# A hybrid decoder layer on eight cores: retention chunks of 128, sums of squares moved off TensorE, four single PSUM side banks

## The chip, the cores and the metric

One Trainium2 chip, eight cores in two dies of four. Each core computes one of eight sequences; nothing is exchanged. The time is that of the slowest core, in device microseconds. All runs named here gave correct results.

The program runs in two states. In a **fast** run the cores have a mean granted TensorE clock that is mostly near 0.993 of full speed. In a **slow** run one die or both are granted less, down to 0.81, and the time is up to 19% longer. The verdict (faster, same, slower) uses fast runs alone. I also use the dies that were left alone: a die whose four cores all show a clock above 0.988 is called **undisturbed**, and its value is the span of its slowest core. Spans are some 2 us under the time.

## The reference, cut to what matters

```python
h = rmsnorm(x);  q_a,k_a,v_a,q_r,k_r,v_r,g_r,z_a,z_r = split(h @ w_in)      # 1024 -> 9472
A = sliding_window_attention(q_a, k_a, v_a)      # window 128, blocks of 128, a sink per head
R = silu(g_r) * rms_group_norm(retention(q_r, k_r, v_r))   # 4 heads, 256 x 512 state, decay gamma
x = x + (sigmoid(z_a) * (A @ w_ba) + sigmoid(z_r) * (R @ w_br)) @ w_out
x = x + (silu(g @ w_gate) * (g @ w_up)) @ w_down,   g = rmsnorm(x)          # FFN of 2816
```

Sequence length 8192, 16 tiles of 512 tokens per core. Retention is computed chunk by chunk with a running state, so the chunk length is the kernel's choice.

## The kernel before

The program lists its operations once, tile by tile: phase A (projections), side (attention and retention), phase F (the FFN of the tile before), phase G (gates, branches, output). A small list scheduler in the kernel file then orders each engine's stream, so side matmuls are fitted between the dense ones of A and F. Dense matmuls use four PSUM banks, side matmuls the other four, here as two double ones. Cut to the parts that the change touches:

```python
PP = Pool("PP", [pp[:, i, :] for i in range(2)])            # two side buffers of 1024 columns

def norm_fm(src, Rsrc, dst, Rdst, gain):                    # RMS norm, features on partitions
    pb = Buf(PP)
    for j in range(4):
        sq = Buf(T16);  act(sq.ap, src[:, 2*j:2*j+2, :], AF.Square, 1024)
        # two matmuls by a matrix of ones: 8 of 512 columns per norm
        S.op("pe", [mm(pb.ap[:, 0:512], ones, sq.ap[:, i*512:(i+1)*512], ...) for i in range(2)])
    ...
def ret_out(t, cc, h, inn):                                 # chunk cc of 256 tokens, head h
    for d in range(4):
        mm(oo(0, 256), vr[c0], inn[:, 0:256])               # inner part, first 128 keys
        mm(oo(128, 256), vr[c1], inn[:, 256:384])           # inner part, second 128 keys
        for dt in range(2): mm(oo(0, 256), Db[h, dt, d], qrT[:, 2*h+dt, 256 tokens])   # state part
    act(sq.ap, po.ap, AF.Square, 1024)
def ret_norm(t, cc, h, po, sq):                             # epsilon and four squares by ones
    fns = [mm(pb.ap[:, 0:256], ones, epsr[:, h, :])] + [mm(pb.ap[:, 0:256], ones, sq[d]) for d in range(4)]
def side(t):
    for (c, eg), (cc, h) in zip([(c, eg) for c in range(4) for eg in range(2)],
                                [(cc, h) for cc in range(2) for h in range(4)]):
        inn = ret_inner(t, cc, h);  km = ret_ktm(t, cc, h)
        pP, pC = attn_scores(t, c, eg);  attn_pv(t, c, eg, pP, pC)   # four pairs of half-array matmuls
        po, sq = ret_out(t, cc, h, inn);  ret_norm(t, cc, h, po, sq);  ret_upd(t, cc, h, km)
```

Weights come from HBM as float32. In the first pass GpSimd issues loads that cast to bf16 into a ring of seven units; each unit is then written back to a bf16 scratch, from which later passes load.

## Time and profile before

| | value |
|---|---|
| the three runs | 5723.11, 5725.18 and 6009.57 us |
| median of the three | 5725.18 us |
| profiled run | 5725.64 us, all clocks 0.991 to 0.994 |
| middle tile | 344.9 us on an undisturbed core, TensorE busy throughout |
| first output tile leaves | 623 to 646 us |

### The profile page before, as it was taken

Reading aid. Unit: us, or ns where it says so; the run is one execution under the profiler, and the core shown is the slowest. Engines: PE = TensorE matmul, PEld = TensorE weight load, DVE = VectorE, ACT = ScalarE, POOL = GpSimd, SP = SyncE. Lnnn points to the kernel's source line nnn. Section 1 sums busy time; section 2 is a strip of 40 time slices with the busy share of each in tenths; the row PEclk is TensorE's granted clock in tenths of the full one; section 3 lists DMA queues with packets and bytes.
Section 4 is the critical chain, followed back from the end, with each engine's and each line's share of the span. In section 5 each row is a group of like instructions: output and inputs, shape, how many; then the busy total and the mean of one; then the engine's idle time right before and its main releaser. Section 6 shows DMA issues by size and latency. Waiting matters only on the chain.

```text
span 5724.1 us, 68116 instructions; the slowest of 8 cores (5698.5 to 5724.1 us)
## 1 busy us (share of the span) xinstructions
PE 5524.7 (97%) x27957; PEld 2606.3 (46%) x28508; DVE 2451.2 (43%) x3550; ACT 2976.4 (52%) x4524; POOL 517.1 (9%) x461
## 2 busy tenths in 40 slices
PE   5788899999999999999999999999999999999999
PEld 2334344444444444444444444444444444444444
DVE  2425344353443535435353443535435344443533
ACT  2636345564454645545565454645546555455643
POOL 2021010100101001020010101001020010101000
PEclk9899999999999999999999999999999999999999
DMA  8676844435354354544535454353544535454353
GB/s 188 145 200 154 223 137 156 156 118 188 129 173 149 120 184 129 173 141 146 165 119 184 133 168 148 121 184 129 173 144 133 173 125 178 138 158 152 113 181 129
DMA packets 241080, 881.13 MB, mean 154 GB/s; under 512 B 26881, under 2 KB 26881, under 8 KB 240641
## 3 DMA queue, kind: packets, MB, share of 16 engines
q1 hardware_dynamic: 228386, 831.65, 44.6%
q0 software_dynamic: 12384, 45.09, 5.1%
q8 instruction: 225, 3.69, 0.3%
q14 instruction: 85, 0.70, 0.0%
HBM read 843.08 MB, written 78.64 MB: 161 GB/s over the span
## 4 chain that ended last, share of the span: by engine, by line
PE 91%; DMA 5%; ACT 2%; DVE 1%; issue 1%; POOL 0%; SPq 0%; POOLq 0%
PE pd L513 79%; PE pp L513 12%; DMA ring<-wpk 2%; ACT s L491 1%; DMA xs<-xT 1%; DMA ring<-wscr 1%; DMA wscr<-ring 1%; PE pp L745 0%; DMA retT<-cb 0%; ACT d L491 0%; DVE d L499 0%; DVE h L502 0%; DVE retT L499 0%; DVE Wst L502 0%; DVE qaT L499 0%
## 5 line engine op out<-in xcount | busy, mean ns | idle before, releaser
L513 PE MATMUL pd<-h,ring 128*128 128x512 bf16 x12589 | 2959.7, 380 | 46.8 <-issue 10.5
L513 PEld LDWEIGHTS pd<-h,ring 128*128 128x128 bf16 x12928 | 1233.6, 98 | 1514.1 <-issue 106.0
L491 ACT ACTIVATE d<-pd 128x512 f32<-128x512 f32 x864 | 509.5, 590 | 1348.0 <-PE pd L513 1344.6
L499 DVE TENSOR_TENSOR d<-pd,d 128x512 f32<-128x512 f32 x736 | 508.4, 691 | 1374.3 <-ACT d L491 793.5
L491 ACT ACTIVATE d<-d,cst_sb 128x512 f32<-128x512 f32 x864 | 623.1, 721 | 25.6
L513 PE MATMUL pd<-actb,ring 128*128 128x512 bf16 x2765 | 613.2, 380 | 13.4 <-DMA ring<-wpk 10.7
L491 ACT ACTIVATE d<-d 128x512 f32<-128x512 f32 x864 | 542.1, 627 | 22.1
L513 PE MATMUL pd<-ring,h 128*128 128x512 bf16 (+1 forms) x2506 | 500.7, 350 | 17.4 <-DMA ring<-wpk 14.5
L513 PE MATMUL pd<-retT,ring 128*128 128x512 bf16 x2015 | 461.6, 379 | 9.1 <-DMA ring<-wpk 7.3
L491 ACT ACTIVATE s<-pp 128x1024 bf16<-128x1024 f32 (+2 forms) x512 | 382.6, 755 | 163.3 <-PE pp L513 159.9
L499 POOL TENSOR_TENSOR qrT<-actb,d 128x512 bf16<-128x512 f32 x112 | 141.6, 1264 | 3579.8 <-DVE d L499 3579.7
L491 ACT ACTIVATE xs<-pd,cst_sb 128x512 bf16<-128x512 f32 x256 | 175.8, 687 | 497.6 <-PE pd L513 497.1
L513 PEld LDWEIGHTS pd<-actb,ring 128*128 128x128 bf16 x2816 | 275.2, 98 | 346.6 <-DMA ring<-wpk 15.5
L499 DVE TENSOR_TENSOR x<-pd,x 128x512 f32<-128x512 f32 x256 | 177.0, 691 | 585.5 <-PE pd L513 583.6
L499 DVE TENSOR_TENSOR actb<-pd,d 128x512 bf16<-128x512 f32 (+1 forms) x480 | 331.3, 690 | 179.0 <-PE pd L513 106.7
L513 PE MATMUL pp<-s,cb_sb 128*128 128x256 bf16 (+2 forms) x1423 | 309.1, 345 | 54.3 <-ACT mprev L491 34.5
L513 PEld LDWEIGHTS pd<-ring,h 128*128 128x128 bf16 x2560 | 233.6, 99 | 266.3 <-DMA ring<-wpk 16.9
L499 DVE TENSOR_TENSOR d<-pd,actb 128x512 f32<-128x512 f32 x512 | 329.0, 685 | 19.5 <-PE pd L513 8.5
L502 DVE SCALAR_TENSOR_TENSOR qaT<-pd,cst_sb,s 128x512 bf16<-128x512 f32 x128 | 95.5, 746 | 540.1 <-ACT s L491 540.1
L513 PEld LDWEIGHTS pd<-retT,ring 128*128 128x128 bf16 x2048 | 199.8, 98 | 250.5 <-DMA ring<-wpk 10.2
L491 ACT ACTIVATE s<-pp,cst_sb 128x512 f32<-128x512 f32 (+1 forms) x302 | 257.9, 855 | 62.2 <-PE pp L513 61.9
L499 POOL TENSOR_TENSOR krT<-d 128x512 bf16<-128x512 f32 x128 | 160.0, 1272 | 1084.0 <-DVE d L499 1084.0
(54 smaller groups left out, 3901.1 us busy)
## 6 DMA issues: line engine op xcount, KB each, us to landing
ring<-wscr SPq DMA_DIRECT2D x1290, 512.0 KB, 3.6
ring<-wpk POOLq DMA_DIRECT2D x86, 512.0 KB, 14.6
wscr<-ring SPq DMA_DIRECT2D x86, 512.0 KB, 12.3
xs<-xT SPq DMA_DIRECT2D x64, 512.0 KB, 5.7
x<-xT SPq DMA_DIRECT2D x64, 512.0 KB, 5.2
out<-x SPq DMA_DIRECT2D x64, 512.0 KB, 4.1
actb<-cs SPq DMA_DIRECT2D x16, 512.0 KB, 6.1
retT<-cb SPq DMA_DIRECT2D x1, 1024.0 KB, 26.5
```

What stands on the lines that cost most here:

```text
L491: return e.activation(out(), in_(), func, scale=scale, **kw)
L499: return S.op(eng, lambda e: e.tensor_tensor(out(), a(), b(), op), dur, reads, writes, cls=cls)
L502: return S.op("dve", lambda e: e.scalar_tensor_tensor(out(), a(), sc, b(), op0, op1), 0.067 + n / 960.0, reads, writes, cls=cls)
L513: return lambda e: e.matmul(out(), w(), r(), start=st, stop=sp)
```

## The change

The intent is to take array columns off TensorE, which is full, and give the small sums to engines that have room: retention chunks of 128 instead of 256, sums of squares added on GpSimd before one matmul by ones, softmax denominators from one VectorE sum. Four single side banks replace two double ones. The side jobs go by head pair. Half of the FFN weight units skip the write-back in the first pass and are cast again in the second. Since GpSimd now computes in several steps, two lines of the scheduler also make it wait, by semaphore, before it overwrites data of its own earlier instructions; they are not shown. The core of the diff, cut:

```diff
-        PP = Pool("PP", [pp[:, i, :] for i in range(2)])
+        PP = Pool("PP", [pp[:, i, :] for i in range(4)])          # pp is now [128, 4, 512]
 # RMS norms: after the first tiles, GpSimd adds the eight squares, one matmul by ones
+                lo, hi = sq.ap[:, 0:512], sq.ap[:, 512:1024]
+                acc = actb[:, 10, :];  tt("pool", acc, lo, hi, ALU.add, 512, ...)   # ... six more adds
+                        S.op("pe", mm(b.ap, ones, ss.ap[:, 0:512], True, True), ...)
+            norm_fm(xs, ..., g1, t <= 2)                            # True: the old way, on TensorE
+            norm_fm(x2, ..., g2, t == ntiles - 1 or t == 0)
 # softmax denominators
+            if t <= 1: return pP, pC, None
+            tt("dve", pS.ap, pP.ap, pC.ap, ALU.add, 1024, ...)      # then one pair by ones instead of two
 # retention: chunks of 128 tokens, two heads per job
-                fns.append(mm(oo(128, 256), vr[:, c1, ...], inn.ap[:, 256:384], ...))
-                        fns.append(mm(oo(0, 256), Db[...], qrT[:, 2 * h + dt, cc * 256:(cc + 1) * 256], ...))
+                        fns.append(mm(oo, Db[...], qrT[:, 2 * h + dt, c * 128:(c + 1) * 128], ...))
 # retention norm
+            if t <= 1: return po, sq
+            tt("pool", qf.ap, sq.ap[:, 0:256], sq.ap[:, 256:512], ALU.add, 256, [sq], [qf])
+            tt("pool", qf.ap[:, 0:128], qf.ap[:, 0:128], qf.ap[:, 128:256], ALU.add, 128, ...)
+            tt("pool", sb_.ap, qf.ap[:, 0:128], epsf[:, h, :], ALU.add, 128, ...)
-            fns = [ones x epsr] + [ones x sq[d] for d in range(4)]  # 5 matmuls of 256 columns
+                fns = [mm(pb.ap[:, 0:128], ones, sb_.ap, True, True)]
 # order of the side jobs
-            for (c, eg), (cc, h) in zip(jobs_a, jobs_r):
+            for eg in range(2):                                     # head pair 0,1 or 2,3
+                for c in range(4):
 # FFN weights: odd units are cast again in the second pass and written back only there
-        WF = Stream(NU_A)
+        WF = Stream(NU_A, True)
+                    late = self.half and u % 2 == 1
+                    if self.npass == 0 or (late and self.npass == 1):  # cast load
+                        if self.npass == (1 if late else 0):           # write back
```

## The prediction

> **What bounds the kernel now.** I read the page first: busy shares, then the waits of TensorE by stretch, then the timeline inside one stretch, then the groups by shape for what the side engines would pay.
>
> The page's first part, and two stretches of about one 512-token tile each in the middle, with the stretch views of the start below them (columns: stretch, its length, busy microseconds and instructions per engine, granted clock, DMA share, GB/s):
>
> ```profile
> PE 5524.7 (97%) x27957; PEld 2606.3 (46%) x28508; DVE 2451.2 (43%) x3550; ACT 2976.4 (52%) x4524; POOL 517.1 (9%) x461
> ```
> ```profile
> 1038.00:1382.00 344.00, 341.26 (x1745) 162.00 (x1779) 152.40 (x221) 185.27 (x283) 29.30 (x23) 1.00 0.46 151
> 1382.00:1726.00 344.00, 341.48 (x1747) 162.24 (x1780) 151.91 (x221) 184.52 (x282) 29.27 (x23) 1.00 0.47 151
> ```
> ```profile
> 34.50:134.50 100.00, 77.08 (x328) 33.17 (x335) 29.15 (x45) 27.99 (x44) 23.33 (x27) 0.90 0.82 188
> 134.50:236.30 101.80, 69.32 (x388) 32.72 (x394) 45.13 (x62) 53.48 (x73) 10.15 (x13) 0.84 0.47 115
> ...
> 547.00:640.00 93.00, 77.67 (x338) 33.09 (x344) 27.64 (x40) 23.63 (x35) 7.39 (x14) 0.98 1.02 229
> ```
>
> TensorE is full in a middle tile (341 of 344) while ScalarE is half used and GpSimd a tenth. Only the first 700 us have holes: the side work of tile 0 (134 to 236, low clock as well) and the first pass over the FFN weights (547 to 640, DMA share 1.02). The waits of TensorE say the same. First the largest ones of 0 to 800 us, then all of 800 to 5350 us:
>
> ```profile
> PE pd L513 <- DMA ring<-wpk: 37.0, 23, 8.5
> PE pp L513 <- ACT mprev L491: 34.5, 1, 34.5
> PE pp L513 <- ACT s L491: 25.7, 26, 2.4
> PE pp L513 <- DVE qaT L499: 13.1, 8, 2.1
> ```
> ```profile
> PE pd L513 <- issue: 9.3, 59, 0.2
> PE pp L513 <- ACT s L491: 8.5, 11, 1.5
> ```
>
> So 13 tiles have 18 us of waits together: every array column removed there is time removed, until something else takes its place. What a column costs is read from starts in the timeline (first column):
>
> ```profile
> 2559.14 0.33 PE L513 MATMUL pp<-s,xs 128*128 128x256 bf16 x2
> 2559.31 0.38 PE L513 MATMUL pp<-qrT,Db 128*128 128x256 bf16 x2
> ...
> 2560.68 1.03 PE L513 MATMUL pd<-ring,h 128*128 128x512 bf16 x4
> 2561.63 0.41 PE L513 MATMUL pp<-s,vx 128*64 128x512 bf16 x2
> 2561.87 0.38 PE L513 MATMUL pp<-s,cb_sb 128*64 128x512 bf16 x2
> ...
> 2562.62 2.76 PE L513 MATMUL pd<-ring,h 128*128 128x512 bf16 x11
> ```
>
> From 2559.14 to 2560.68 sixteen matmuls of retention run (12 of 256 columns, 4 of 128) in 1.54 us, so there is no dependence stall between matmuls into the same bank. Start to start, single records are 216 ns for 512 columns, 109 for 256, 56 for 128. The pairs of half-array matmuls start 3 to 4 ns apart: a pair costs one. Entering the half-array form costs: the four dense matmuls at 2560.68 should end their slot at 2561.54, the pair starts at 2561.63. Over a whole core I count 576 such changes, median excess 95 ns, or 36 per tile (18 excursions), 3.4 us per tile.
>
> **What the Trainium skill says.** "TensorE: Matmul & The Clock Gate", section "Wait — 56ns, not 53.3ns?", gives N / 2.4 GHz + 2.5 ns: 215.8, 109.2, 55.8 ns. The trace agrees to a nanosecond, so I price with it. (The same page, "Back-to-back issue gap", gives about 81 ns at N=128 for streams with weight loads; the trace shows 56 with a new weight each time. The measurement decides; it matters, since the change makes many 128-column matmuls.) "TensorEngine Tiling (Array Packing)", "Key Properties", says that a change of tiling mode drains TensorE: that is the 95 ns above. "SBUF — State Buffer", "Who interferes with whom", says that a VectorE instruction with two SBUF inputs contends with a GpSimd instruction that reads SBUF; no row of the kernel before isolates this, and the change adds GpSimd reads.
>
> **The change part by part.** TensorE now: dense 512-column matmuls per tile 808 on the normalized input, 128 for the retention values, 176+128+64+64 for the others, 1368 x 0.2158 = 295.2 us, plus 32 of 128 columns. All 16 tiles with the side work sum to 5447 us of array time; my count from the records of a complete core gives the same 5447.2. Removed per tile, from tile 2 on:
> - Retention chunk 256 to 128, scores inside a chunk: 8 x (2 x 0.1092 + 2 x 0.0558) = 2.64 becomes 8 x 4 x 0.0558 = 1.79: -0.85.
> - Retention output: 8 x 4 x (3 x 0.1092 + 0.0558) = 12.27 becomes 16 x 12 x 0.0558 = 10.71: -1.55. (The strip of the triangle above the diagonal block goes.)
> - Retention norm: five 256-column matmuls by ones per job, 8 x 5 x 0.1092 = 4.37, become 16 x 0.0558 = 0.89, because GpSimd adds the four squares and epsilon first: -3.47.
> - Softmax denominators: 4 pairs per job become 3 (VectorE adds the two probability tiles first): -8 x 0.2158 = -1.73.
> - The two RMS norms: 8 matmuls each become 1 (GpSimd adds): -2 x 7 x 0.2158 = -3.02.
> - State update: 8 x 4 against 16 x 2 matmuls of 512: nothing.
>
> Sum 10.6 us per tile. The first two tiles keep the old norms and denominators, and norm 1 of tiles 0 to 2 and norm 2 of tiles 0 and 15 stay on TensorE. So: 14 x 7.60 + 27 x 1.51 + 2 x 2.3 = 151.8; less 3.4 for the first chunk, which now skips only 128 tokens of state work, and four more updates: **148 us** off TensorE, all where it waits for nothing.
>
> Added elsewhere per tile, with these rows (busy us in total, mean ns of one):
>
> ```profile
> L491 ACT ACTIVATE Db<-Wst 128x1024 bf16<-128x1024 f32 x124 | 130.2, 1050 | 163.7 <-DVE Wst L502 155.5 <-DVE Wst L506 8.1
> L502 DVE SCALAR_TENSOR_TENSOR Wst<-Wst,pp 128x1024 f32<-128x1024 f32 x120 | 145.5, 1213 | 9.2 <-PE pp L513 9.2
> L499 POOL TENSOR_TENSOR krT<-d 128x512 bf16<-128x512 f32 x128 | 160.0, 1272 | 1084.0 <-DVE d L499 1084.0
> ```
>
> ScalarE: 8 more state copies x 1.05 = 8.4, exponentials in halves +3.6, squares and norm chains in halves about +4: +16, so 185 to 201 of some 333. VectorE: updates 32 x about 0.7 against 8 x 1.213, +12.7; probability sums 8 x about 0.78, +6; +19 with the rest: 152 to 171. GpSimd: 1272 ns per 512 gives about 2.5 ns a column; 16 x (256+128+128 columns, some 1.5 us with fixed cost) = 24 and 16 x 1.25 = 20: 29 to 73. None becomes full, all estimates from the rows above. They are beside TensorE, unless a chain gets too long.
>
> PSUM: two double banks become four single ones. Jobs now go by head pair, chunk after chunk, so half of them need only heads 0 and 1 and can start before the projections end. That matters for tile 0, where nothing else covers them: they start at 130 us and eight take 110 us. I put a gain of 25 us on it (four of eight jobs partly under the weight loads of the projections; shorter pieces). Weight stream of the FFN: in the first pass every second unit isn't written back, but cast again in the second pass. DMA time per unit from the queue shares: casts 5.1% of 5724 us / 86 = 3.4 us, a write-back about 1.6; 5.0 becomes 4.2 on average against 3.45 of TensorE for 16 matmuls. In the DMA-full stretch that saves about 12 us. The second pass has room (DMA share 0.46).
>
> Costs: the current and previous scores need two banks each, besides one for the inner scores; four banks hold only one set, so I expect fewer score pairs back to back: 22 excursions for 18, +4 x 0.19 = 0.8 us per tile, +12. New small waits (GpSimd chain before the norm, second pass): +10.
>
> Sum: 5725 - 148 - 25 - 12 + 12 + 10 = **5562 us**, -2.8%.
>
> **Rivals.** (1) The side chain becomes the bound. Each state now passes through update, VectorE, ScalarE and back four times a tile, in neighbouring jobs; GpSimd puts three dependent adds before the norm, holding a bank meanwhile. For it: one job already takes 14.9 us, waiting mostly on ScalarE and VectorE. Against: 8 x 14.9 = 119 us lie in about 150 us of FFN and side work, they start earlier, and my chain from update to new state is about 4 us (estimate) against 14 per job. At 20 us a job the gate phase waits some 10 us a tile, 150 in all: about 5710, no gain. (2) Mode changes go to 24 excursions and more: +18, near 5570. (3) GpSimd blocks: its queue is in order, and in tile 2 cast loads that wait for a ring slot stand before the adds; or it contends with VectorE. One tile of trouble: +10; every norm late: TensorE waits on GpSimd, 20 to 60. (4) The start doesn't move since weights are the limit there: 5599. (5) The start gains more, since half its holes go: 5520.
>
> **Range and chances.** The 148 us are counted, and alone give -2.6%; the start and the new waits are judged, each within some 40 us. Range 5515 to 5625. The line for 2% is 5611: rivals 1 or 3 in half strength, with a start that gains nothing, cross it. Faster 0.88, same 0.11, slower 0.01.
>
> **What would show it.** TensorE's busy time near 5375, 96 to 97% of the span; one middle tile in about 334 us; ones-matmuls of 256 columns gone from tile 2 on; ScalarE near 3220, VectorE near 2730, GpSimd near 1150. In the first 700 us smaller waits on the weights and on side work. I am wrong if middle tiles show waits of TensorE on GpSimd, or on ScalarE and VectorE in retention and gate phase, of more than 3 us per tile, or if 128-column matmuls take much over 56 ns, or if mode changes exceed 50 per tile.

## More of the kernel before

The groups of TensorE on a core whose records are complete (core 7) show what the change goes for: matmuls whose only use is to add over partitions. Columns: line, engine, operation, output and inputs, array form, shape, count, then busy us and mean ns, then idle time before them.

```profile
L513 PE MATMUL pp<-s,cb_sb 128*128 128x512 bf16 x400 | 132.4, 385 | 49.9 <-ACT mprev L491 34.2 <-ACT s L491 14.1 <-DVE retT L499 1.3
L513 PE MATMUL pp<-s,cb_sb 128*64 128x512 bf16 x512 | 100.2, 388 | 0.0
L513 PE MATMUL pp<-s,cb_sb 128*128 128x256 bf16 x512 | 78.8, 278 | 0.0
L513 PE MATMUL pp<-cb_sb 128*128 128x256 bf16 x128 | 35.3, 276 | 12.2 <-DVE qaT L499 12.2
```

The 400 are 256 for the RMS norms and 144 for the query and key norms; the 512 of half-array form are the softmax denominators; the last two lines are the retention norm. The mean of 385 ns is the length of one record, whose end is modelled. The records overlap, and 216 ns from start to start is what each costs.

The end of each tile is read from the issues of its last output store (first column, core 7):

```profile
633.02 1.10 SPq L509 DMA_DIRECT2D out<-x  x1
...
992.72 0.34 SPq L509 DMA_DIRECT2D out<-x  x1
...
1337.59 0.39 SPq L509 DMA_DIRECT2D out<-x  x1
```

The first interval, 359.7 us, still contains start effects. From the second on an interval is 344.9 us.

## The result

Fast runs: 5562.68, 5565.53 and 5570.65 us. **The ratio of fast runs to fast runs is 0.9718, 95% interval 0.9701 to 0.9736: faster.** A ratio here is the mean time of one kernel's fast runs over that of the other's of the same rounds, so not quite the ratio of quoted medians. On undisturbed dies the changed kernel has a median of 5562.9 us (15 dies). All outputs are right.

But only 3 of its 14 runs were fast. The median of all 14 is 6052.38 us, and that of the 15 of the kernel before in the same rounds 6009.57. Per tile the two traces leave no doubt. The first part of the page, then a middle tile of each kernel (core 7: before, then changed; columns as in the prediction):

```profile
PE 5428.6 (98%) x28871; PEld 2522.9 (45%) x28871; DVE 2708.7 (49%) x4171; ACT 3118.1 (56%) x5290; POOL 1144.8 (21%) x1338
```
```profile
1000.00:1344.90 344.90, 344.90 (x1787) 162.96 (x1786) 153.09 (x223) 185.93 (x283) 29.26 (x23) 1.00 0.46 152
```
```profile
1000.00:1335.70 335.70, 335.63 (x1797) 156.48 (x1795) 170.13 (x262) 194.30 (x332) 73.95 (x85) 1.00 0.48 156
```

TensorE is full in both, and the tile is 9.2 us shorter (9.8 in the mean of all cores over tiles 4 to 13, 345.5 to 335.7, since some tiles of before had small waits). VectorE, ScalarE and GpSimd took 17, 8 and 45 us more per tile with no effect on its length: between 1000 and 5100 us this core's waits of TensorE list nothing at all. The groups of the changed kernel that answer to those shown of before:

```profile
L521 PE MATMUL pp<-s,cb_sb 128*128 128x512 bf16 x211 | 79.0, 394 | 55.7 <-ACT mprev L499 34.9 <-ACT s L499 17.3 <-POOL s L507 3.4
L521 PE MATMUL pp<-s,cb_sb 128*64 128x512 bf16 x288 | 53.5, 388 | 0.0
...
L521 PE MATMUL pp<-b,cb_sb 128*128 128x128 bf16 x224 | 49.8, 222 | 0.0
```

The counts are the ones that the change asks for: 400 - 27 x 7 = 211, and 512 - 14 x 16 = 288. The retention norm is one matmul of 128 columns. A head's output, from the timeline of the changed kernel:

```profile
2499.92 0.22 PE L521 MATMUL pp<-i,xs 128*128 128x128 bf16 x1
2499.97 0.28 PE L521 MATMUL pp<-qrT,Db 128*128 128x128 bf16 x2
...
2500.59 2.75 PE L521 MATMUL pd<-h,ring 128*128 128x512 bf16 x12
```

Twelve matmuls of 128 columns start within 0.67 us, 56 ns each, each with a new weight. The short ones run at the priced rate.

The start moved too (last output stores of the first three tiles, core 7):

```profile
602.80 0.34 SPq L517 DMA_DIRECT2D out<-x  x1
...
952.36 0.56 SPq L517 DMA_DIRECT2D out<-x  x1
...
1291.52 0.34 SPq L517 DMA_DIRECT2D out<-x  x1
```

Averaged over the eight cores, the first output tile leaves at 602.1 us instead of 635.8, the next two intervals are 347.3 and 340.3 instead of 355.1 and 345.2, and the changed kernel keeps 335.7 from there on. Of the 34 us at the start, 26 are idle time of TensorE before the first output tile (132 to 106 us in the mean of the cores). Another 7 are granted clock: in the start the clock records have stretches of 3.4 to 13.7 us at 0.5, and what they take adds up to 34 us before and 27 after. Tiles 2 and 3 don't have their full gain yet. The largest waits of TensorE between 700 and 1000 us in the changed kernel are:

```profile
PE pp L521 <- POOL s L507: 3.4, 1, 3.4
PE pp L521 <- DVE s L507: 2.2, 1, 2.2
```

The first is the norm ahead of tile 3. Its GpSimd accumulator shares memory with the FFN activations, so its adds can't begin until the down projection has read them; on core 4 they run from 951.7 to 961.0 us. That holds for the later tiles too. But there 44 matmuls stand before the norm's matmul in TensorE's order (9.5 us), and here only 28 (6.0 us). All the waits of this stretch come to 7.0 us, and at 895 us, right after some of them, the clock records grant 0.5 for 6.8 us. Before, this stretch had one wait of 0.4 us.

### The profile page after: what moved, and what is told of

It is laid out like the page before. It is cut to its first block, busy times and chain, and to the rows that moved or that the text cites. A ratio compares the mean times of both kernels' runs of the same rounds, so it can differ in the third digit from the quotient of the medians.

```text
span 5561.1 us, 71882 instructions; the slowest of 8 cores (5549.4 to 5561.1 us)
## 1 busy us (share of the span) xinstructions
PE 5428.6 (98%) x28871; PEld 2522.9 (45%) x28871; DVE 2708.7 (49%) x4171; ACT 3118.1 (56%) x5290; POOL 1144.8 (21%) x1338
## 4 chain that ended last, share of the span: by engine, by line
PE 93%; ACT 2%; DVE 2%; DMA 2%; issue 0%; POOL 0%; SPq 0%
PE pd L521 83%; PE pp L521 10%; ACT s L499 1%; DMA ring<-wpk 1%; DVE h L510 1%; PE pp L784 1%; DMA retT<-cb 0%; ACT d L499 0%; ACT Db L499 0%; ACT vx L499 0%; DVE Wst L510 0%; DMA ring<-wscr 0%; DVE qaT L510 0%; DVE d L507 0%; DVE qaT L507 0%
## 5 line engine op out<-in xcount | busy, mean ns | idle before, releaser
L521 PE MATMUL pd<-h,ring 128*128 128x512 bf16 x12928 | 3031.8, 380 | 16.1 <-DVE h L510 10.0
L507 POOL TENSOR_TENSOR q<-q 128x256 f32<-128x256 bf16 x448 | 288.9, 645 | 1230.1 <-ACT q L499 1212.6
L521 PE MATMUL pd<-ring,h 128*128 128x512 bf16 (+1 forms) x2560 | 508.3, 351 | 15.1 <-DMA ring<-wpk 15.1
L521 PEld LDWEIGHTS pd<-actb,ring 128*128 128x128 bf16 x2816 | 275.5, 98 | 335.7 <-DMA ring<-wpk 3.7
L499 ACT ACTIVATE s<-pp 128x512 bf16<-128x512 f32 (+2 forms) x640 | 282.8, 464 | 130.1 <-PE pp L521 128.4
L510 DVE SCALAR_TENSOR_TENSOR Wst<-Wst,pp 128x512 f32<-128x512 f32 x496 | 326.2, 682 | 44.1 <-PE pp L521 42.9
L499 ACT ACTIVATE Db<-Wst 128x1024 bf16<-128x1024 f32 x252 | 264.2, 1049 | 92.9 <-DVE Wst L510 90.0
L499 ACT ACTIVATE s<-pp,cst_sb 128x512 bf16<-128x512 f32 (+1 forms) x428 | 286.4, 679 | 53.3 <-PE pp L521 53.2
```

Of the source, the lines that this page charges most:

```text
L499: return e.activation(out(), in_(), func, scale=scale, **kw)
L507: return S.op(eng, lambda e: e.tensor_tensor(out(), a(), b(), op), dur, reads, writes, cls=cls)
L510: return S.op("dve", lambda e: e.scalar_tensor_tensor(out(), a(), sc, b(), op0, op1), 0.067 + n / 960.0, reads, writes, cls=cls)
L521: return lambda e: e.matmul(out(), w(), r(), start=st, stop=sp)
```

## Experiments

Each run edits the changed kernel, unless said otherwise, and ran beside the kernel before on the same chip. I compare undisturbed dies and intervals of the trace. The base is 5562.9 us in all, 602 us for the first output tile, then 347.3, 340.3 and 335.7. These early figures vary: five profiles whose program is the same up to the first output tile have 602 to 607 us, and the changed kernel run again had 344.9 for the second figure. The kernel before had 5718 to 5721 on the undisturbed dies of these chips.

**The norms back on TensorE.**
```diff
-norm_fm(xs, ..., g1, t <= 2)                       +norm_fm(xs, ..., g1, True)
-norm_fm(x2, ..., g2, t == ntiles - 1 or t == 0)    +norm_fm(x2, ..., g2, True)
```

> The changed kernel with one part undone: the sums of squares of the two RMS norms back on TensorE for every tile (8 matmuls of 512 columns each instead of 1; the GpSimd adds go). Theory (array columns are the time, everything else hidden): a middle tile +3.0 us over the 335.7 of the changed kernel, so 338.7; 27 norms x 1.51 = +41 us in all, about 5606 in the fast state. Rival (the GpSimd adds had given part of it back through waits): less than +25 us. Rival (the gain comes from the start, not from columns): +10 or less.

Measured: middle tile 338.4 (+2.7), undisturbed dies 5598.9 (+36). This fits the columns being the time. The third figure, the interval of tile 3, falls from 340.3 to 338.3 although work was added, since the late norm of tile 3 is gone: about 5 us less than the columns say. A middle tile is also 0.35 us short of its columns, which no run explains, and the first output tile left 4.5 us later, within the spread of that start.

**The retention norm back on TensorE.**
```diff
-            if t <= 1:            # in ret_out and in ret_norm
+            if True:
```

> The changed kernel with the retention norm on TensorE in every tile, as its first two tiles have it (5 matmuls of 128 columns per head and chunk instead of 1; the three GpSimd adds go). Theory: a middle tile +16 x 4 x 0.0558 = +3.6, so 339.3; in all +50 us, about 5615. Rival (the chain of three GpSimd adds holds a PSUM bank and costs TensorE waits): less than +30, or even none.

Measured: middle tile 338.65 (+2.95), in all 5593.7 (+31), near the edge of the rival's range. The changes of array form in the trace fell from 754 to 670, since the schedule packed side groups differently: 84 x 0.0955 = 8 us. The interval of 347.3 became 340.3 in spite of the added columns. Between 600 and 1000 us core 7 has no listed wait of TensorE at all, where the changed kernel has 11.1 us (4.1 of them on weights). So in tile 2 the GpSimd chain does cost time, some 8 to 10 us with the spread of that interval, while in middle tiles it costs none.

**The denominators back on TensorE.**
```diff
-            if t <= 1:
+            if True:
                 return pP, pC, None
```

> The changed kernel with the softmax denominators summed on TensorE from both probability tiles in every tile (4 pairs of half-array matmuls per job instead of 3; VectorE's add of the two tiles goes). Theory: a middle tile +8 x 0.2158 = +1.7, so 337.4; in all +24 us, about 5590. Rival (VectorE is the tighter engine and the added sum costs as much as it saves): within 8 us of the changed kernel.

Measured: middle tile 337.4 (+1.7 as worked out), in all 5582.0 (+19); again the interval of tile 2 is shorter (340.5 on die 0; die 1 was slow in this profile). So VectorE is not the tighter engine in middle tiles. Both runs agree that tile 2's side work is where new waits sit.

**All FFN units written back.**
```diff
-Stream(NU_A, True)
+Stream(NU_A, False)
```

> The changed kernel with every FFN weight unit written back in the first pass again, and none cast a second time. Theory (the first FFN pass is limited by DMA, a unit costing 5.0 instead of 4.2 us of DMA time): the middle tiles stay at 335.7, the first output tile leaves some 12 us later than the 603 to 606 us of the changed kernel; in all +12, about 5577. Rival (the first pass waits for side work, not for weights): 0 to 3 us.

Measured: first output tile at 620 (+18), then 345.7 and 335.5 on the die with full clock: tile 3 loses its extra 5 us. In all 5573.0 (+10). On core 7 the waits of TensorE on cast loads before 700 us are, in this run and then in the changed kernel:

```profile
PE pd L521 <- DMA ring<-wpk: 39.6, 21, 6.1
```
```profile
PE pd L521 <- DMA ring<-wpk: 27.0, 11, 6.8
```

In the mean of the cores all waits on weights before 700 us are 46.0 us here and 28.8 in the changed kernel. So weights limited the first pass. The second casts are not free: tiles 2 and 3 are 1.6 and 4.9 us longer with them. By which path is not shown. Tile 3's extra time is also gone in the next run, which keeps the casts.

**Side jobs chunk by chunk.**
```diff
-            for eg in range(2):
-                for c in range(4):
+            for c in range(4):
+                for eg in range(2):
```

> The changed kernel with its side jobs in the old order: chunk after chunk with both head pairs in each, instead of one head pair through all four chunks. Nothing is added or removed on any engine. Theory (the head-pair order lets four of the eight jobs of tile 0 start under the weight loads): the first output tile leaves 15 to 25 us later than the 602 us of the changed kernel, middle tiles stay at 335.7, in all about 5580. Rival (the start gains through the smaller PSUM pieces alone): within 5 us of the changed kernel.

Measured: first output tile at 616 (+14; 615 on die 0, since die 1 had stretches at clock 0.8125 in this start), third figure 335.5, in all 5575.0 (+12). With the spread of that start, the order by head pair is worth 12 to 14 us there, a little under the expectation. Only about half of it is time that TensorE waits, which is what the theory was about: on die 0 the idle time before the first output tile is 112 us instead of 105, and the stretches at clock 0.5 take 34.5 us instead of 26.5. Together with the 18 us of the run before, the order accounts for nearly all of the 34 us by which the start moved. By subtraction little is left for the smaller PSUM pieces by themselves, but no run undoes the four banks, and the two parts need not simply add.

**GpSimd adds three times over.**
```diff
-            tt("pool", qf.ap, sq.ap[:, 0:256], sq.ap[:, 256:512], ALU.add, 256, [sq], [qf])
+            for _ in range(3):
+                tt("pool", qf.ap, sq.ap[:, 0:256], sq.ap[:, 256:512], ALU.add, 256, [sq], [qf])
```

> The changed kernel with the first of the three GpSimd adds of each retention norm done three times over (the same result): 16 x 2 x 0.645 = 20.6 us more GpSimd work per tile, and 1.3 us more in the chain before each norm. Theory (hidden): middle tiles stay at 335.7 within 1 us; only tiles 2 and 3, where GpSimd also casts weights, may lose up to 10 us. Rival (the GpSimd chain is nearly on the path): middle tiles +5 or more, the whole +70.

Measured: middle tile 335.8, in all 5563.8 (+1). In middle tiles GpSimd's work and the longer chain are hidden, with room to spare.

**Scores in one group.** A job's scores against the previous and the current key block are two groups of two half-array matmuls. Here they are one of four, taking all four side banks:
```diff
-    def sc(slot, ...): pbs = [Buf(PP), Buf(PP)]; S.op("pe", [mm(... kv=0), mm(... kv=1)], ...)
+    bank = {(s, kv): Buf(PP) for s in slots for kv in range(2)}
+    S.op("pe", [mm(bank[s, kv].ap, kTr[...s], qaT[...]) for s in slots for kv in range(2)], ...)
```

> The changed kernel with the scores against the previous and the current key block in one group of four half-array matmuls that takes all four PSUM side banks, so that TensorE changes its form less often. Theory (each change costs 0.0955 us and nothing else does): changes go from 754 to about 520, 47 to 32 per tile, middle tiles 335.7 - 1.4 = 334.3, in all -15 to -22 us, about 5543. Rival (waiting for four free banks at once stretches a side job from 15 to over 18 us): middle tiles unchanged or longer, the start longer by 10.

Measured: form changes 754 to 512, but the middle tile is 335.35 (-0.35 instead of -1.4), the first output tile is at 615 (+13), and in all it is 5567.3 (+4). The saving is there and came back as a new wait, one per tile (waits of TensorE, 1000 to 5100 us, core 7):

```profile
PE pp L521 <- DVE s L507: 15.2, 12, 1.3
```

It is at the first side job. The timeline there, VectorE's masks of the two probability tiles and GpSimd under them:

```profile
1146.94 2.94 POOL L507 TENSOR_TENSOR krT<-d 128x512 bf16<-128x512 f32 x2 [12.39 <-DVE d L507]
1147.37 1.38 DVE L507 TENSOR_TENSOR s<-s,mprev 128x1024 bf16<-128x1024 bf16 x1
1148.68 1.75 DVE L507 TENSOR_TENSOR s<-s,cb_sb 128x1024 bf16<-128x1024 bf16 x1
...
1152.61 0.62 PE L521 MATMUL pp<-s,vx 128*64 128x512 bf16 x4 [1.27 <-DVE s L507]
```

Elsewhere in a tile, with GpSimd idle, each of these masks takes 0.69 us (the 2498.70 and 2500.82 us of the changed kernel). Under GpSimd's rotation work they take 1.38 and 1.75, and VectorE also has its own rotation products to do. No run takes the GpSimd work away, so how much of the wait each of the two causes stays open.

**Scores in one group, but not in the first job nor in tiles 0 and 1.**
```diff
+            merged = t >= 2 and (c > 0 or eg > 0)
```

> The changed kernel with the scores of both key blocks in one group, as before, but not in the first side job of a tile (where the merged group ran into a VectorE that is busy with the rotation) and not in tiles 0 and 1. Theory (the mode changes were saved, and one new wait of 1.3 us per tile took the saving back): no wait of TensorE on VectorE in middle tiles, middle tiles 335.7 - 7 x 0.21 = 334.2 us, in all about -18, 5545 on undisturbed cores. Rival (the wait moves to the second job): 335.3 as in the run with all jobs merged.

Measured: the wait is gone (one of 0.2 us per tile is left, on VectorE's `retT`). With 558 form changes the middle tile is 334.5 on the die with full clock, -1.2 where 14 changes fewer per tile are priced at -1.3. That die has 5538.5 in all (-24, more than expected, since the late norm of tile 3 is gone too: 334.5 in the third figure). The other die shows a clock of 0.984 to 0.986 in each run in which it is not slow, and 337.1 per tile; more on that below.

**Constants first.** Both kernels wait 34 us for the first matmul, for a load of constants of 1 MB (26 us to land). In the changed kernel 1152 of its 2048 columns are in use.
```diff
-        load_xs(0);  dma("sp", stg[:, 0:2048], cb_d, ...)
+        dma("sp", stg[:, 0:1152], cb_d[:, 0:1152], ...);  load_xs(0)
-        ... mask and sinks -> [R_c]       +        ... mask and sinks -> [R_mp], awaited by attention alone
```

> The changed kernel with the load of the constants put ahead of the load of x and cut to the columns in use, and the mask and sinks no longer waited for by the first matmul. Both kernels wait 34 us before the first matmul. Theory: the first matmul starts at 15 to 22 us, and half of that is kept, since the projections of tile 0 then wait for their weights: the first output tile leaves 5 to 12 us earlier than at 602, in all about 5555. Rival (the weights set the pace from the start): within 3 us of the changed kernel.

Measured: first matmul at 15 us, first output tile at 595 (-7), in all 5555.6 (-7), fast runs at 0.9728 of the kernel before. Of 19 us at the front, 7 are kept. The trace gives another reason than the weights that both theories named. The loads of x now land behind the constants, and ScalarE squares x from 15.0 to 30.6 us instead of 8.4 to 24.6 (core 7). So the norm ends late, and the first projection matmul starts at 36.5 us instead of 42.5: only 6 us are left there already. The waits on weights before 700 us hardly change (28.8 to 27.0 us in the mean of the cores).

**All of it together:** constants first, merged scores as above, denominators on TensorE in tile 2 as well, and the norm ahead of tile 3 too.
```diff
-            if t <= 1:  # denominators        +            if t <= 2:
-norm_fm(xs, ..., g1, t <= 2)                  +norm_fm(xs, ..., g1, t <= 3)
```

> Constants first, scores merged in all but the first job from tile 2 on, denominators on TensorE also in tile 2, and the norm ahead of tile 3 on TensorE too. Theory (the gains lie in different stretches and add up): first matmul at 15 us, first output tile at 595, the next two intervals 341 and 336 to 338 instead of 348 and 340, middle tiles 334.2; in all -7 - 11 - 18 = -36 against the changed kernel, about 5527 on undisturbed cores, ratio to before about 0.966. Rival (the schedule shifts, and small waits come back elsewhere): 5545 or more.

Measured, on the chip of the run with merged later jobs: on the full-clock die 5527.1, just what was added up, with 338, 334.2 and 334.5 for the intervals, the first two 2 to 4 us better than expected. But the other die ran near 0.986, so the fast runs read 5565.73 to 5570.76 and the ratio 0.9726. The stretches of a core of that die at the same place of a tile, then of a core of the full-clock die (the column before the last two is the granted clock):

```profile
1288.00:1303.00 15.00, 15.00 (x59) 6.19 (x58) 10.70 (x17) 11.08 (x18) 0.00 (x0) 0.82 0.48 152
```
```profile
1288.00:1303.00 15.00, 15.00 (x71) 6.83 (x70) 7.77 (x12) 12.40 (x21) 0.00 (x0) 1.00 0.47 166
```

Once per tile, at the start of the gate phase, the clock records grant 0.8125 for 15.1 us. 15.1 x 0.1875 = 2.8 us, and the tile is 2.6 us longer.

**Before, with the norms on GpSimd alone.** The one part put into the kernel before:
```diff
-def norm_fm(src, Rsrc, dst, Rdst, gain):  # 8 matmuls by ones
+def norm_fm(..., quick):                  # as in the change: seven GpSimd adds, one matmul (and its two scheduler lines)
```

> The kernel before with one part of the change alone: the squares of the two RMS norms added on GpSimd, one matmul of 512 columns instead of 8 (the first tiles and the last excepted, as in the change). Theory (TensorE's columns are the time, whatever else is there): middle tiles 344.9 - 3.0 = 341.9, in all -36 to -41. Rival (two PSUM side banks only, so the longer norm chain blocks side work): middle tiles 344 or more, or waits of TensorE on GpSimd.

Measured on the full-clock die: middle tile 342.2 (-2.7), in all 5688.2 against 5718.2 (-30), no waits on GpSimd. The part is worth the same per tile in either kernel. Its fast runs read 5715 to 5716, ratio 0.9983 (0.9961 to 1.0005, unclear), because the other die again ran near 0.985, with the same stretches of 15.1 us at 0.8125: without the cores' clocks this would have passed for "no effect". On that die most of the gain really is lost: 5710 to 5715 us, where the kernel before took 5717 to 5732 in the runs in which the die was not slow. Its cores were then at 0.987 to 0.993 with the kernel before, and at 0.983 to 0.989 with each of the three edited kernels that ran on this chip.

**The changed kernel again, and the combined one, on another chip.** Does the change bring the slow state on, and do the stretches of 15.1 us (bursts) follow the kernel?

> The changed kernel itself, beside the kernel before on the same chip, to count states. Theory (the slow state falls on any kernel alike): of its runs as many are slow as of the kernel before in the same job, some 6 in 10; fast runs at 5560 to 5570, ratio near 0.972. Rival (a TensorE with fewer waits trips the limit more often): clearly more slow runs than before, or fast runs with short stretches at clock 0.81 in middle tiles that the kernel before does not have on the same die.

> The combined kernel once more, beside the changed kernel. Theory: 5527 on undisturbed cores, 35 us under the changed kernel, ratio to before 0.966; the stretches of 15 us at clock 0.81 once per tile that it showed on one die of another chip come with that die and not with the kernel, so they are absent here or present in the changed kernel too. Rival (they come with the denser schedule): present here on a die where the changed kernel has none, middle tiles at 337.

Measured: the changed kernel has 2 fast runs of 7 (5565.29 and 5599.32, the latter with a die at 0.984), the kernel before 3 of 11. Ratio 0.9754 with a wide interval (0.9683 to 0.9824, unclear), undisturbed dies 5561.7 against 5721.2, which is 0.9721. The combined kernel has 5528.80, 5529.13 and 5548.15, **ratio 0.9677 (0.9637 to 0.9717), faster** than the kernel before; undisturbed dies have 5526.2, 35.5 us (0.6%) under the changed kernel's, and both dies have full clock in two of its three fast runs. So the bursts are not the kernel's alone. They are not the die's alone either: on the die of the other chip the kernel before hardly lost clock. The changed kernel itself did not run on that chip, so whether it would have had them there stays open. Over all jobs, 18 of 51 runs of the kernel before were fast, 5 of 21 of the changed one and 25 of 63 of the other variants. That shows no clear difference, though it couldn't rule out a modest one. What makes a die slow on a given run stays open.

One check across states: slow dies of equal clock keep the gain. With its cores at 0.822 to 0.826 the slow die of the kernel before took 6770.8 and 6780.4 us; the changed one at 0.820 to 0.825 took 6588.2 and 6605.3. The ratio of the means is 0.974, as one would expect where array work is the limit; it is no evidence beyond the fast runs.

## Why the prediction was right or wrong

**The stated time against the median: wrong.** The step that failed is the last one, "Range 5515 to 5625", which weighed only "the start and the new waits" and took for granted, with the sum that began at 5725, that the measured runs would be fast. The runs showed instead that the slow state is the usual one: 11 of the 14 were slow, with the slower die at a clock of 0.82 to 0.93, and their median, 6052, lies outside the range. No term of the sum stands for that. What makes a die slow stays open. The one warning was in hand: the third run of the kernel before, 6009.57. Its median over 51 runs is 6060.6, not 5725. A range for the median would have had to be two ranges with a weight for each state, 5515 to 5625 for fast runs and a second one for slow runs near 5900 to 6600.

**The effect: right.** Fast runs lie at 5563 to 5571, ratio 0.9718 against 5562 / 5725 = 0.9715, class faster, given 0.88. By its own steps:

| step | predicted | measured |
|---|---|---|
| array columns | -148 | -148.7 (matmul counts and widths of a complete core, priced the same way) |
| middle tile | about 334 | 335.7 |
| start, side jobs of tile 0 | -25 | -12 to -14 (order undone), about half of it granted clock |
| FFN write-backs | -12 | -18 at the start, -10 after what tiles 2 and 3 give back |
| form changes | +12, 22 excursions a tile | +17, 754 changes for 576 (about 24) |
| new waits | +10 | the intervals of tiles 2 and 3 are together 16 us over two middle tiles, before they were 10 over; none in middle tiles |

The start was right in sum (34 us at the first output tile against 37). How it is shared stays open. By the two runs that undo a part, the write-backs had more of it than the order. By the waits before 700 us (means of the cores), those on weights fell by 11 us, 39.5 to 28.8, and all others except the one for the constants by 18, 63.8 to 45.4, which is nearer to the prediction. The granted clock, with 7 of the 34 us, is not in the prediction. That both kinds of waits would shrink was one of its signs, and came true. The form changes are my term that was plainly too small; the second rival, 24 excursions, was the right one, and 47 changes a tile stay under the 50 that the prediction set as its limit. The terms overlap a little, so the rows should not be added to the microsecond. Three parts of the middle tile's 9.2 us were undone one by one, 2.7 + 2.95 + 1.7 = 7.35 us; the shorter chunk, 2.4 us by the count, was not undone in any run.

**Busy times.** TensorE's was expected near 5375 and reads 5428.6. Most of that is lost records: the profiled core of before lacks 551 matmuls, and a complete core of it reads 5568.4 where the page reads 5524.7. On core 7, complete in both, the busy time fell by 140 us, 5568.4 to 5428.2. ScalarE was expected near 3220 and reads 3118, since I priced each half-size instruction by its whole length and not by what it adds. VectorE (2730, read 2709) and GpSimd (1150, read 1145) came out.

**The rivals.** The side chain did not become the bound: a middle tile has no wait. Tiles 2 and 3 have waits of about the size that the third rival gave for one tile of trouble. That the order of GpSimd's queue causes them, as it said, is not shown: without the second casts tile 2 still takes 345.7 us, and tile 3's extra time also goes when only the jobs are reordered. The rival that the start would not move is out by the two runs that undo its causes.

## What to carry to other kernels

When one engine is full in the middle of a run and waits for nothing, count what the change takes from it, column by column at the start-to-start rate of the trace: the count came true to a microsecond, the tile to 1.7 us, and what was judged by feel was right only in sum. Before trusting a saving on such an engine, look for the one wait per iteration that gives it back, and where it sits: merging the scores everywhere gained nothing, merging them everywhere but in one job per tile gained 1.2 us a tile. And where a program has two states, predict and compare within a state, read every core's clock, and never let a median over the states stand for the kernel.

## What the Trainium skill lacked or had wrong

- "TensorE: Matmul & The Clock Gate", section "Back-to-back issue gap": about 81 ns per 128-column matmul, and 131 per 512-column one, in a stream with weight loads. Here it is 56 ns with a new weight each time, twelve in 0.67 us, and 216 ns for 512 columns. The page's N / 2.4 + 2.5 holds.
- "TensorEngine Tiling (Array Packing)", section "Key Properties": it says that a change of tiling mode drains TensorE and gives no cost. Here each change has a median excess of 95 to 96 ns, and it is saved only if nothing else becomes late (242 changes fewer, about 1.4 us per tile by that price, 0.35 kept; 196 fewer, 1.3 by that price, 1.2 kept).
- "SBUF — State Buffer", section "Who interferes with whom": its rule on VectorE instructions with two SBUF inputs fits the trace, but it has no figure for such a case. Two masks of 0.69 us took 1.38 and 1.75 while GpSimd was working.
- "TensorE: Matmul & The Clock Gate", section "Seeing it yourself": it expects 13/16 of the clock for sustained dense matmuls on all cores. Here all eight cores ran at 0.993 in fast runs; 0.81 is what the slowest dies had, and on one die it came in bursts of 15.1 us once per tile (0.82 in that stretch). That the state differs from run to run is not on the page.
